# Seven block products in place of eight for the gate and up tiles of a float32 feed-forward on Trainium2

## Chip, cores and metric

The kernel runs on one core of one Trainium2 chip. The metric is device time in microseconds from start to end of one execution; the median of three runs is compared. Engines are called as in the profile: PE (TensorE matmuls), PEld (its weight loads), DVE (VectorE), ACT (ScalarE), POOL (GpSimd), SP (which issues the DMAs).

## What is computed

One block of an encoder: a feed-forward, token mixing (two attention branches, not touched here), a second feed-forward, a final norm. The part that matters:

```python
D_MODEL, SEQ, D_FF = 1024, 512, 2816      # all float32
def swiglu(h, w_in, w_down):
    g, u = jnp.split(h @ w_in, 2, axis=-1)
    return (jax.nn.silu(g) * u) @ w_down
...
h = modulate(rmsnorm(x, g_ffn2), sh3, sc3)
x = x + 0.5 * gt3[:, None, :] * swiglu(h, w_ffn2_in, w_ffn2_down)
return rmsnorm(x, g_final)
```

## The kernel before

Activations lie transposed, features on the 128 partitions, the 512 tokens along the free axis. `h` is eight K-tiles of 128 features (`KD` = 8). The 2816 inner features are 22 tiles (`NP_FF`), and each inner tile needs a gate tile and an up tile of 128 output features, a *pair*.

A float32 product runs as three matmuls (`mm3`): each operand is split into a high part, rounded by a cast on ACT (`wh_`, `f2h`, `hh`), and a low part, the rest, by a subtraction on DVE (`wl_`, `f2l`, `hl`); high*high, high*low and low*high add up in PSUM. So one output tile of `h @ w_in` over all 512 tokens (`proj`) is 8 K-tiles x 3 = 24 matmuls of 512 columns, and a pair is 48.

The second feed-forward (`swiglu(2, ...)`) goes like this. `first_group` makes the first `FIRST` = 3 pairs together, K-tile by K-tile, while `h` is still being formed, in halves of 256 tokens, into six PSUM banks. Then 19 pairs follow one by one: load 512 KB of gate weights (`ws_2g`) and 512 KB of up weights (`ws_2u`), split both, 48 matmuls, and `gated`: Silu on ACT, product on DVE, split into `hh` and `hl`. The inner tiles come in three groups (`THIRDS`: 8, 7 and 7). After each of the first two groups the eight output tiles (*down tiles*, weights `ws_2d`) are multiplied from the group's inner tiles and added to `x` by DVE. The last group's down tiles run in `residual`, the last four (`LAST`) in two halves of 256 tokens, followed by the sums of squares, the final norm and the output.

Nothing in the code is issued in the order in which it is written. `Plan` records all operations and a list scheduler orders them: an operation goes to its engine when its operands and a slot for its result are there, by its priority; `Plan.cost` estimates durations, `LAT` the delays between engines, `CAPS` how many buffers of a kind may live. Each engine then runs its list strictly in order, with semaphore waits. A bank serves one engine at a time. All operations are issued from one helper line, so rows are told apart by the names of tiles.

Of the kernel before, what the change touches and what calls it, by code (L numbers as in the profile page):

```python
# [30 lines left out]
THIRDS = ((0, 8), (8, 15), (15, 22))  # L31
# [15 lines left out]
# the work up to the end of the first projections, in the order of its urgency, and what engines wait for  # L47
# [18 lines left out]
WG_POOL = (1, 3)  # L66
RING = 2
# [3 lines left out]
CAPS = {"x": 4, "x2": 8, "sq": 4, "h": 16, "hid": 20, "sg": 1, "mt0": 2, "mt256": 2, "nrm": 6, "wst": 1, "whi": 7, "wlo": 7,  # L71
# [5 lines left out]
# the mixing: I index scores, A sparse queries, L latents, U latent values, R rotary queries, P query and key  # L77
# pairs, S and W scores and values of a latent head, T top-k, G gates, D and E scores and values of four sparse heads
# [5 lines left out]
# its operations in the order of their urgency, and what engines wait for  # L84
# [29 lines left out]
TINY = {"norm": 16, "top1": 2, "top2": 2, "top3": 2, "mla": 24, "dsa": 24}  # L114
# [14 lines left out]
def _mt(w):  # L129
    """(K, M) -> [M/128][128 partitions of K][K/128][128]"""  # L130
    k, m = w.shape
    return w.reshape(k // P, P, m // P, P).transpose(2, 1, 0, 3)


def _prep(inp):
# [9 lines left out]
    for n in (1, 2):  # L145
# [5 lines left out]
        for t, (lo, hi) in enumerate(THIRDS):  # L151
            a[f"w{n}d{t}"] = wd[:, :, lo:hi].reshape(KD, P, (hi - lo) * P)
# [28 lines left out]
    # rows that mask the first 64 queries of each block from its last 64 keys: queries, keys  # L181
# [20 lines left out]
class View:  # L202
# [31 lines left out]

    def bitcast(self, dt):
        return View(self.buf, self.chain + [("bitcast", dt)], self.p, self.off, self.dims, dt)
# [5 lines left out]
    def box(self):  # L242
        """partitions, columns, and the runs of columns where these have holes"""
# [11 lines left out]
    def real(self):  # L255
        ap = self.buf.base()
        for kind, *a in self.chain:
            if kind == "get":
                ap = ap[a[0]]
            elif kind == "bitcast":  # L260
                ap = ap.bitcast(a[0])
            else:
                ap = ap.rearrange(a[0], **a[1])
# [44 lines left out]
class Clock:  # L308
    """the tensor engine's clock: half as fast after a window in which it did little"""
# [21 lines left out]
# functions of ScalarE by the table that it loads for them  # L331
# [3 lines left out]
class Plan:  # L335
# [27 lines left out]
    def record(self, eng, nc_engine, fn, args, kw):  # L363
# [14 lines left out]
        if op.eng == "pe":  # L378
            # the share of the time in which rows of the array work
# [6 lines left out]
        op.step = self.step  # L386
        deps = {}
# [8 lines left out]
        for v in outs:  # L396
# [40 lines left out]
    def cost(eng, fn, outs, ins, kw, args):  # L437
        """an estimate, for the order alone"""
# [20 lines left out]
    # -- scheduling  # L459
    def order(self):  # L460
# [28 lines left out]
        while len(done) < len(self.ops):  # L489
            best = None  # L490
            for e, lst in ready.items():
# [4 lines left out]
                for op in lst:  # L496
# [4 lines left out]
                    for b in op.banks:  # L501
                        # a bank serves one engine at a time
# [9 lines left out]
                # an engine is not to begin something long just before urgent work  # L512
# [92 lines left out]
class Block:  # L605
# [8 lines left out]
    def small(self, kind, n=4):  # L614
        """per-partition scalars, from a ring of its own for each kind of use"""
# [11 lines left out]
    def later(self):  # L627
        """work that only fills what the rest leaves free"""
# [5 lines left out]
    def urgent(self, *engines):  # L634
        """work that all of the next work waits for"""
# [4 lines left out]
    def split(self, hi, lo, src, engine=None):  # L640
        """hi + lo == src: hi rounded to float32r by ScalarE, the rest by VectorE"""
# [12 lines left out]
    def mm3(self, ps, wh, wl, xh, xl, start, stop, hh=True):  # L654
        mm = self.nc.tensor.matmul
        if hh:
            mm(ps, wh, xh, start=start, stop=False)
        mm(ps, wh, xl, start=False, stop=False)
        mm(ps, wl, xh, start=False, stop=stop)

    def proj(self, w, x, nk, name, tag, cols=ALL):
        """one tile of 128 output features: sum over nk K-tiles"""
# [896 lines left out]
```

## Time and profile before

| | |
|---|---|
| median of three runs | 1181.84 us (1181.27 to 1186.75) |
| span of the profiled execution | 1182.4 us, 0.6 us above that median |
| PE busy, share of the span | 1137.4 us, 96% |
| PEld, DVE, ACT, POOL busy | 949.1, 744.1, 502.6, 123.3 us |
| HBM read / written | 148.11 / 13.63 MB |
| second feed-forward | from about 797 us to the end |

The busy share of PE is an average over stages, so the stretches have to be read by themselves. A matmul's printed duration reaches to its modelled end; back to back they overlap, and the distance from start to start is what counts. DVE and ACT instructions overlap a little in the same way.

### The profile page before, as it was taken

The page shows a single profiled execution, that of the slowest core. Times are in us where ns is not written, and L with a number is a line of the kernel's source. Part 1 is how long each engine was busy: PE and PEld are TensorE (multiplying, and loading weights), DVE is VectorE, ACT ScalarE, POOL GpSimd, SP SyncE. Part 2 cuts the span into 40 slices and gives each one's busy share as a digit, 9 for nine tenths or more (in the row PEclk, how much of TensorE's full clock was granted, in tenths as well). Part 3 has the DMA queues.
Part 4 walks back from the last instruction along what each step waited for, and adds up shares of the span by engine and source line. Part 5 has one row for each costly group of instructions (what it writes and reads, how often), then busy time and mean ns, then how long its engine had stood idle before and what let it go on. Part 6 is the DMA issues. An engine that isn't in the chain of part 4 may idle for free. (4 is left out here: it accounts for less than half of the span.)

```text
span 1182.4 us, 15861 instructions
## 1 busy us (share of the span) xinstructions
PE 1137.4 (96%) x5955; PEld 949.1 (80%) x5957; DVE 744.1 (63%) x1381; ACT 502.6 (43%) x896; POOL 123.3 (10%) x111
## 2 busy tenths in 40 slices
PE   5999999999999999988999999999999999999996
PEld 3878788887877899776888777889988888888886
DVE  8876665547664796899997786848433333333335
ACT  5562413423343256454768777524432222223220
POOL 5120000000000000021235352000000000000000
PEclk8899999999999999999999999999999999999998
DMA  8555566548545753221144256423322332333212
GB/s 292 188 182 180 171 225 194 175 166 271 182 152 184 264 172 121 72 81 65 55 127 123 95 190 209 157 68 112 107 97 99 92 105 78 100 107 100 83 32 71
DMA packets 64543, 163.88 MB, mean 139 GB/s; under 512 B 9762, under 2 KB 21538, under 8 KB 64467
## 3 DMA queue, kind: packets, MB, share of 16 engines
q1 hardware_dynamic: 64466, 162.88, 41.7%
q8 instruction: 46, 0.75, 0.3%
q14 instruction: 31, 0.25, 0.1%
HBM read 148.11 MB, written 13.63 MB: 137 GB/s over the span
## 5 line engine op out<-in xcount | busy, mean ns | idle before, releaser
L602 DVE CUSTOM_DVE_ANT_0 junk<-ada,sc,vecs 128x1024 bf16<-128x1024 f32 x66 | 84.5, 1281 | 28.6 <-DMA ada<-in_w_ada_dram 28.4
L602 PE MATMUL bank<-hmh,wh_ib 128*128 128x512 f32 x200 | 79.8, 400 | 1.7 <-ACT wh_ib L602 1.7
L602 PE MATMUL bank<-hmh,wl_ib 128*128 128x512 f32 x200 | 80.2, 404 | 0.3 <-POOL wl_ib L602 0.3
L602 PE MATMUL bank<-hml,wh_ib 128*128 128x512 f32 x200 | 79.5, 398 | 0.0
L602 DVE TENSOR_TENSOR wl_2d<-ws_2d,wh_2d 128x896 fp32r<-128x896 f32 (+1 forms) x24 | 27.3, 1137 | 75.2 <-ACT wh_2d L602 75.2
L602 PE MATMUL bank<-hl,wh_2d 128*128 128x512 f32 (+1 forms) x204 | 73.6, 361 | 0.0
L602 PE MATMUL bank<-hh,wh_2d 128*128 128x512 f32 (+1 forms) x204 | 73.5, 360 | 0.0
L602 PE MATMUL bank<-hh,wl_2d 128*128 128x512 f32 (+1 forms) x204 | 73.4, 360 | 0.0
L602 PE MATMUL bank<-hh,wh_1d 128*128 128x512 f32 (+1 forms) x197 | 72.6, 369 | 0.0
L602 PE MATMUL bank<-hl,wh_1d 128*128 128x512 f32 (+1 forms) x197 | 72.4, 367 | 0.0
L602 PE MATMUL bank<-hh,wl_1d 128*128 128x512 f32 (+1 forms) x197 | 72.2, 366 | 0.0
L602 DVE TENSOR_TENSOR wl_2g<-ws_2g,wh_2g 128x1024 fp32r<-128x1024 f32 x19 | 23.3, 1225 | 60.1 <-ACT wh_2g L602 60.1
L602 DVE SCALAR_TENSOR_TENSOR x<-bank,gt,x 128x512 f32<-128x512 f32 (+1 forms) x66 | 44.0, 666 | 25.5 <-PE bank L602 25.4
L602 PE MATMUL bank<-f1h,wh_1g 128*128 128x512 f32 x152 | 59.5, 391 | 0.0
L602 PE MATMUL bank<-f1l,wh_1g 128*128 128x512 f32 x152 | 59.2, 389 | 0.0
L602 PE MATMUL bank<-f1h,wl_1g 128*128 128x512 f32 x152 | 59.2, 389 | 0.0
L602 PE MATMUL bank<-f2h,wh_2g 128*128 128x512 f32 x152 | 59.1, 389 | 0.0
L602 PE MATMUL bank<-f2l,wh_2g 128*128 128x512 f32 x152 | 59.1, 389 | 0.0
L602 PE MATMUL bank<-f1h,wh_1u 128*128 128x512 f32 x152 | 59.1, 389 | 0.0
L602 PE MATMUL bank<-f1l,wh_1u 128*128 128x512 f32 x152 | 59.1, 389 | 0.0
L602 PE MATMUL bank<-f2h,wl_2g 128*128 128x512 f32 x152 | 59.1, 389 | 0.0
L602 PE MATMUL bank<-f2h,wh_2u 128*128 128x512 f32 x152 | 59.1, 389 | 0.0
(328 smaller groups left out, 3088.2 us busy)
## 6 DMA issues: line engine op xcount, KB each, us to landing
ada<-in_w_ada_dram SPq DMA_DIRECT2D x72, 512.0 KB, 4.5
ws_ib<-in_wib_dram SPq DMA_DIRECT2D x25, 512.0 KB, 3.4
ws_1g<-in_w1b_dram SPq DMA_DIRECT2D x19, 512.0 KB, 3.7
ws_1u<-in_w1b_dram SPq DMA_DIRECT2D x19, 512.0 KB, 3.5
ws_2g<-in_w2b_dram SPq DMA_DIRECT2D x19, 512.0 KB, 3.7
ws_2u<-in_w2b_dram SPq DMA_DIRECT2D x19, 512.0 KB, 3.4
ws_1d<-in_w1d_dram SPq DMA_DIRECT2D x16, 448.0 KB, 3.5
ws_2d<-in_w2d_dram SPq DMA_DIRECT2D x16, 448.0 KB, 3.2
```

What stands on the lines that cost most here:

```text
L602: op.fn(*[real(v) for v in op.args], **{k: real(v) for k, v in op.kw.items()})
```

## The change

Only the second feed-forward changes its arithmetic. A pair is seen as a 2x2 block product: rows gate and up, the sum over the first and the second four K-tiles (1 and 2 below), the tokens in two halves a and b. Winograd's form of Strassen's method makes its four results from seven block products, each 4 K-tiles x 3 = 12 matmuls of 256 columns, so 84 of them. It needs sums of the weight blocks (`wc_`: `s12`, `s34`, formed for each pair) and of the blocks of `h` (`f2t`, T0 to T3, formed once by `token_combinations`). Per pair four operands are split: the gate weights `a` (1024 columns), `t` = s34 (1024), `s` = s12 (1024) and `b` = the second up half (512). The products add up in two banks, A and C, with ACT copying intermediate sums of A to SBUF (`v`, `v2`) between products, and DVE adding or subtracting to get `g` and `u`.

Further: the K-tiles of the first group go 0, 4, 1, 5, ..., without the six opening matmuls over all 512 columns; pair loads wait for a matmul of the third K-tile (`fast_from`); five groups of inner tiles (4, 4, 4, 5, 5); a group's eight down tiles are recorded between the pairs of the next group. In the planner, the cost of an unnamed float32r matmul becomes 13.4 ns + columns / 2.4, which can also shift the order in the first feed-forward.

```diff
-THIRDS = ((0, 8), (8, 15), (15, 22))
+GROUPS = {1: ((0, 8), (8, 15), (15, 22)), 2: ((0, 4), (4, 8), (8, 12), (12, 17), (17, 22))}
...
+FAST_FROM = 2
...
+        if eng == "pe" and op.step is None and mv.dt == F32R:
+            op.cost = 13.4 + mv.n / 2.4
...
+        ks = [k // 2 + KD // 2 * (k % 2) for k in range(KD)] if fast is not None else list(range(KD))
...
+                    behind = halves[i][-2] if fast is not None else None
...
+                        if fast is not None:
+                            self.mm3(first[m][:w, cols], wh[:, c], wl[:, c], xh, xl, start, k == ks[-1] and cols.stop == S,
+                                     skip_group_check=True)
+                            continue
...
+            if fast is not None and k == ks[FAST_FROM]:
+                self.fast_from = nc.last_pe
+        if fast is not None:
+            for k in range(KD // 2):
+                fast.append(self.token_combinations(f"{name}t{k}", site, k, kept[k], kept[k + KD // 2]))
...
+        V.tensor_tensor(t13[:, 0], m0[:, a], m0[:, b], op=ALU.subtract)
+        V.scalar_tensor_tensor(t13[:, 1], m0[:, b], d, m1[:, b], op0=ALU.subtract, op1=ALU.subtract)
+        V.scalar_tensor_tensor(t24[:, 0], t13[:, 1], sh0, m0[:, a], op0=ALU.subtract, op1=ALU.subtract)
+        V.scalar_tensor_tensor(t24[:, 1], m1[:, a], sh1, t24[:, 0], op0=ALU.add, op1=ALU.add)
+        out = []
+        for i, t in enumerate((t13, t24)):
+            hi, lo = (self.g(f"{name}{c}{i}", F32R, shape=(P, 2, S // 2), tag="th") for c in "hl")
+            self.split(hi, lo, t)
+            out += [(hi[:, e], lo[:, e]) for e in range(2)]
...
+        with nc.after(self.fast_from):
+            nc.sync.dma_start(w0, src0)
+            nc.sync.dma_start(w21, src1[:, lo_])
+            nc.sync.dma_start(w22, src1[:, hi_])
...
+        p0 = parts("a", w0, "w")
+        V.tensor_tensor(s34[:, lo_], w0[:, lo_], w21, op=ALU.add)
+        V.tensor_tensor(s12[:, hi_], w21, w22, op=ALU.add)
+        V.tensor_tensor(s12[:, lo_], s12[:, hi_], w0[:, lo_], op=ALU.add)
+        V.tensor_tensor(s34[:, hi_], w0[:, hi_], s12[:, lo_], op=ALU.add)
+        p34 = parts("t", s34, "w")
+        p12 = parts("s", s12, "w")
+        p22 = parts("b", w22, "v")
+        A, C = (self.bank(f"{n}_{name}", "mm") for n in "ac")
...
+            for k in range(K4):
+                self.mm3(ps, *w[k], *x[k], start and k == 0, k == K4 - 1, skip_group_check=True)
...
+        product(A[:, a], cols(p0, 0), quarter(0, 0), True)
+        nc.scalar.copy(v[:, 0], A[:, a])
+        product(C[:, a], cols(p34, 0), T[1], True)
+        product(A[:, a], cols(p12, 0), T[2])
+        nc.scalar.copy(v[:, 1], A[:, a])
+        product(C[:, b], cols(p0, S), quarter(K4, 0))
+        product(A[:, a], cols(p12, S), T[0])
+        nc.scalar.copy(v2[:, 0], A[:, a])
+        V.tensor_tensor(g[:, 0], v[:, 0], C[:, b], op=ALU.add)
+        V.tensor_tensor(u[:, 1], v2[:, 0], C[:, a], op=ALU.subtract)
+        product(A[:, a], cols(p34, S), quarter(K4, 1))
+        product(C[:, a], cols(p22, 0), T[3])
+        V.tensor_tensor(u[:, 0], v[:, 1], C[:, a], op=ALU.subtract)
+        return g, u, A[:, a]
...
+        def gated_fast(i):
+            src = A[f"w{n}b"][i - FIRST]
+            g, u, c12 = self.fast_pair(f"f{i}", src[0], src[1], h, combos)
+            nc.scalar.activation(g[:, 0], g[:, 0], AF.Silu)
+            nc.scalar.activation(g[:, 1], c12, AF.Silu)
+            nc.vector.scalar_tensor_tensor(g, u, -1.0, g, op0=ALU.mult, op1=ALU.mult)
+            hi, lo = self.g(f"hh{n}_{i}", F32R, tag="hid"), self.g(f"hl{n}_{i}", F32R, tag="hid")
+            e = lambda t: t.rearrange("p (e t) -> p e t", e=2)
+            nc.scalar.copy(e(hi), g)
+            nc.vector.tensor_tensor(e(lo), g, e(hi).bitcast(F32), op=ALU.subtract)
+            hid[i] = (hi, lo)
...
+            for j, i in enumerate(new):
+                hidden(i)
+                while before and len(before) > KD - KD * (j + 1) // len(new):
+                    before.pop(0)()
...
+                before = [lambda d=d, tile=tile, weights=weights: tile(d, weights(d)) for d in range(KD)]
```

Three places show what the planner makes of it. Rows are in the order in which an engine runs them; the wait of an instruction stands behind it.

First, PE where one output ends and the next begins. Before, the up tile of pair 4 ends in one bank and the gate tile of pair 5 starts in another:

```order
L602 MATMUL bank0_179<-f2h7_7911,wh_2u4_7977 128x512
L602 MATMUL bank0_179<-f2l7_7931,wh_2u4_7977 128x512
L602 MATMUL bank0_179<-f2h7_7911,wl_2u4_7989 128x512
L602 MATMUL bank7_186<-f2h0_6715,wh_2g5_8010 128x512 [waits Activation_49]
L602 MATMUL bank7_186<-f2l0_7661,wh_2g5_8010 128x512
L602 MATMUL bank7_186<-f2h0_6715,wl_2g5_8024 128x512
```

Now, in pair 8, the fifth product (`f8s`) ends in bank 188, three matmuls of a down tile follow in bank 183, and the sixth product (`f8t`) goes on in bank 188:

```order
L612 MATMUL bank5_188<-f2t3h0_8072,wh_f8s_8892 128x256
L612 MATMUL bank5_188<-f2t3l0_8089,wh_f8s_8892 128x256
L612 MATMUL bank5_188<-f2t3h0_8072,wl_f8s_8911 128x256
L612 MATMUL bank0_183<-hh2_4_8470,wh_2d1_0_8928 128x512
L612 MATMUL bank0_183<-hl2_4_8481,wh_2d1_0_8928 128x512
L612 MATMUL bank0_183<-hh2_4_8470,wl_2d1_0_8936 128x512 [waits DVE_49]
L612 MATMUL bank5_188<-f2h4_7669,wh_f8t_8829 128x256 [waits Activation_49]
L612 MATMUL bank5_188<-f2l4_7681,wh_f8t_8829 128x256
```

The sixth product waits for ACT, which first has to copy the fifth sum out of the same bank; the three down matmuls stand between.

Second, DVE while the first group runs, just before the first pair. Before, it makes the low parts of `h` and of the weights of pairs 3 to 5:

```order
L602 SCALAR_TENSOR_TENSOR f2l7_7931<-mf2h7_0_7902,mod_73,f2h7_7911 128x256 [waits Activation_49]
L602 SCALAR_TENSOR_TENSOR f2l7_7931<-mf2h7_256_7908,mod_73,f2h7_7911 128x256 [waits Activation_49]
L602 TENSOR_TENSOR wl_2u3_7943<-ws_2u3_7868,wh_2u3_7924 128x1024 [waits DMAHW1_49,PE_49,Activation_49]
L602 TENSOR_TENSOR wl_2g4_7962<-ws_2g4_7898,wh_2g4_7950 128x1024 [waits DMAHW2_49,PE_49,Activation_49]
L602 TENSOR_TENSOR wl_2u4_7989<-ws_2u4_7934,wh_2u4_7977 128x1024 [waits DMAHW3_49,PE_49,Activation_49]
L602 TENSOR_TENSOR wl_2g5_8024<-ws_2g5_7972,wh_2g5_8010 128x1024 [waits DMAHW4_49,DVE_49,Activation_49]
```

Now it is at the last block sums of `h` (`f2t3`) and the weight sums of pair 3 (`wc_f30` is s12, `wc_f31` is s34), and the product `sg2_0` of the first group's first pair stands ahead of `wl_f3t`, which the second product of pair 3 needs:

```order
L612 TENSOR_TENSOR wc_f31_8101<-ws_f30_7914,ws_f31_7924 128x512 [waits DMAHW2_49,PE_49]
L612 TENSOR_TENSOR wc_f30_8110<-ws_f31_7924,ws_f32_7932 128x512 [waits DMAHW3_49,PE_49]
L612 TENSOR_TENSOR f2t3l1_8118<-f2t32_8083,f2t3h1_8104 128x512 [waits Activation_49]
L612 TENSOR_TENSOR wc_f30_8110<-wc_f30_8110,ws_f30_7914 128x512 [waits DVE_49]
L612 TENSOR_TENSOR wl_f3b_8132<-ws_f32_7932,wh_f3b_8003 128x512
L612 TENSOR_TENSOR wc_f31_8101<-ws_f30_7914,wc_f30_8110 128x512 [waits DVE_49]
L612 TENSOR_TENSOR sg2_0_8137<-sg2_0_8137,bank6_189 128x512 [waits PE_49,Activation_49]
L612 TENSOR_TENSOR wc_f41_8157<-ws_f40_7939,ws_f41_7950 128x512 [waits DMAHW5_49,DMAHW4_49]
L612 TENSOR_TENSOR wl_f3t_8170<-wc_f31_8101,wh_f3t_8150 128x1024 [waits Activation_49]
```

Twenty-eight operations on 256 columns and further ones, counted in the prediction, stand between the first multiplication of `x` by the second half's norm and this last row.

Third, DVE in a later pair, where before it had four operations a pair. Now, while pair 7 is multiplied:

```order
L612 TENSOR_TENSOR g_f7_8895<-v_f7_8850,bank2_185 128x256 [waits PE_49,Activation_49]
L612 TENSOR_TENSOR wl_f8s_8911<-wc_f80_8784,wh_f8s_8892 128x1024 [waits PE_49,Activation_49]
L612 TENSOR_TENSOR u_f7_8924<-v2_f7_8913,bank2_185 128x256 [waits Activation_49]
L612 TENSOR_TENSOR wl_2d1_0_8936<-ws_2d1_0_8897,wh_2d1_0_8928 128x512 [waits DMAHW7_49,PE_49,Activation_49]
L612 TENSOR_TENSOR wc_f90_8951<-ws_f91_8614,ws_f92_8622 128x512 [waits DMAHW1_49,DVE_49]
L612 TENSOR_TENSOR wl_f9b_8960<-ws_f92_8622,wh_f9b_8944 128x512 [waits Activation_49]
L612 TENSOR_TENSOR u_f7_8924<-v_f7_8850,bank2_185 128x256 [waits PE_49]
L612 TENSOR_TENSOR wc_f90_8951<-wc_f90_8951,ws_f90_8748 128x512 [waits DVE_49]
L612 SCALAR_TENSOR_TENSOR g_f7_8895<-u_f7_8924,g_f7_8895 128x512 [waits DVE_49]
L612 TENSOR_TENSOR wc_f91_8875<-ws_f90_8748,wc_f90_8951 128x512 [waits DVE_49]
L612 SCALAR_TENSOR_TENSOR x2_6_6927<-bank1_184,gt_75,x2_6_6927 128x512 [waits PE_49]
L612 TENSOR_TENSOR hl2_7_8988<-g_f7_8895,hh2_7_8980 128x512 [waits Activation_49]
```

The parts of pair 8 and the sums of pair 9 are made in between, one pair or two ahead of PE.

## Rows read from the trace of the kernel before

**Rows 1.** Cores: span and mean granted clock.
```profile
core 0: 1182.4 us, clock 0.988
```

**Rows 2.** Stretches: length; PE, PEld, DVE, ACT, POOL busy (instructions); clock; DMA; GB/s.
```profile
790.00:841.10 51.10, 51.10 (x412) 50.35 (x411) 34.39 (x80) 21.39 (x34) 0.00 (x0) 1.00 0.34 104
841.10:1160.00 318.90, 318.90 (x1454) 266.10 (x1453) 113.93 (x130) 86.38 (x107) 0.00 (x0) 1.00 0.27 88
...
1160.00:1170.20 10.20, 10.20 (x86) 10.07 (x84) 7.93 (x27) 1.25 (x3) 0.00 (x0) 1.00 0.15 51
1170.20:1182.40 12.20, 1.96 (x8) 1.02 (x6) 5.78 (x21) 0.42 (x1) 0.00 (x0) 0.63 0.38 129
```

**Rows 3.** Waits from 800 to 1160: us in total, times, longest us.
```profile
DVE wl_2d L602 <- ACT wh_2d L602: 75.2, 24, 4.5
...
ACT wh_2g L602 <- DMA ws_2g<-in_w2b_dram: 57.0, 19, 4.5
```

**Rows 4.** Timeline of PE, 822 to 841: start us, us, what.
```profile
821.79 0.28 PE L602 MATMUL bank<-f2l,wh_f 128*128 128x256 f32 x1
...
840.99 0.28 PE L602 MATMUL bank<-f2h,wl_f 128*128 128x256 f32 x1
841.11 0.40 PE L602 MATMUL bank<-f2h,wh_2g 128*128 128x512 f32 x1
```

**Rows 5.** Timeline of PE, 910 to 955.
```profile
909.82 0.39 PE L602 MATMUL bank<-hh,wh_2d 128*128 128x512 f32 x1
...
954.25 0.39 PE L602 MATMUL bank<-f2l,wh_2g 128*128 128x512 f32 x1
```

**Rows 6.** Groups by shape, PE from 841 to 1171: busy us, mean ns.
```profile
L602 PE MATMUL bank<-f2h,wh_2g 128*128 128x512 f32 x152 | 59.1, 389 | 0.0
...
L602 PE MATMUL bank<-hh,wh_2d 128*128 128x512 f32 x148 | 57.6, 389 | 0.0
```

**Rows 7.** Groups by shape, DVE from 795 on: busy us, mean ns, idle before.
```profile
L602 DVE TENSOR_TENSOR wl_2g<-ws_2g,wh_2g 128x1024 fp32r<-128x1024 f32 x19 | 23.3, 1225 | 60.1 <-ACT wh_2g L602 60.1
...
L602 DVE TENSOR_TENSOR hl<-sg,hh 128x512 fp32r<-128x512 f32 x22 | 15.2, 692 | 13.7 <-ACT hh L602 13.7
...
L602 DVE SCALAR_TENSOR_TENSOR x<-bank,gt,x 128x512 f32<-128x512 f32 x20 | 14.9, 746 | 9.0 <-PE bank L602 9.0
...
L602 DVE TENSOR_TENSOR acc_n<-acc_n,sq_n 128x256 f32<-128x256 f32 x12 | 5.1, 423 | 2.4 <-ACT sq_n L602 2.3
```

**Rows 8.** Timeline of DVE, 792 to 850 and at the end.
```profile
814.21 0.87 DVE L602 SCALAR_TENSOR_TENSOR mf2h<-x,a,bank 128x256 f32<-128x256 f32 x2 [0.59 <-PE bank L602]
...
816.07 1.26 DVE L602 SCALAR_TENSOR_TENSOR mf2h<-x,a,bank 128x256 f32<-128x256 f32 x3
...
1175.74 3.22 DVE L602 SCALAR_TENSOR_TENSOR o<-x,vecs,bank 128x256 f32<-128x256 f32 x8 [1.31 <-PE bank L602]
```

**Rows 9.** Groups by shape, ACT: busy us, mean ns, idle before.
```profile
L602 ACT CAST wh_2g<-ws_2g 128x1024 fp32r<-128x1024 f32 x19 | 19.9, 1050 | 57.0 <-DMA ws_2g<-in_w2b_dram 57.0
...
L602 ACT CAST pBh<-bank 128x256 fp32r<-128x256 f32 x8 | 3.0, 374 | 6.3 <-PE bank L602 5.2 <-DVE tiny_dsa L602 1.0
```

**Rows 10.** Timelines, hand-offs: PE to ACT, then ACT to PE.
```profile
857.23 0.39 PE L602 MATMUL bank<-f2h,wl_2g 128*128 128x512 f32 x1
...
857.66 0.60 ACT L602 ACTIVATE sg<-bank 128x512 f32<-128x512 f32 x1 [1.07 <-PE bank L602]
...
530.94 1.04 ACT L602 CAST wh_ib<-ws_ib 128x1024 fp32r<-128x1024 f32 x1
...
532.03 0.50 PE L602 MATMUL bank<-hmh,wh_ib 128*128 128x512 f32 x1 [1.67 <-ACT wh_ib L602]
532.37 0.39 PE L602 MATMUL bank<-hml,wh_ib 128*128 128x512 f32 x1
```

**Rows 11.** Timeline of ACT, 836 to 845.
```profile
839.51 0.60 ACT L602 ACTIVATE sg<-bank 128x512 f32<-128x512 f32 x1 [1.10 <-PE bank L602]
```

**Rows 12.** DMA issues after 700: count, KB each, median us to landing.
```profile
ws_2g<-in_w2b_dram SPq DMA_DIRECT2D x19, 512.0 KB, 3.7
```

More of the change, by code (lines that the diff above doesn't have):

```diff
@@ L764, in residual, with modulated, first_group @@
         return r
-    def modulated(self, h, x, r, a, sh, cols):
+    def modulated(self, h, x, r, a, sh, cols, kept=None, behind=None):
         nc = self.nc
-        hi, lo = (t[:, cols] for t in h)
-        t = self.g(f"m{h[0].name}_{cols.start}", shape=(P, cols.stop - cols.start), tag=f"mt{cols.start}")
-        nc.vector.scalar_tensor_tensor(t, x[:, cols], a, r[:, cols], op0=ALU.mult, op1=ALU.mult)
+        hi, lo = h
+        t = kept[:, cols] if kept is not None else self.g(f"m{h[0].buf.name}_{cols.start}", shape=(P, cols.stop - cols.start), tag=f"mt{cols.start}")
+        with nc.after(behind, True):
+            nc.vector.scalar_tensor_tensor(t, x[:, cols], a, r[:, cols], op0=ALU.mult, op1=ALU.mult)
         nc.scalar.activation(hi, t, AF.Identity, bias=sh)
-        nc.vector.scalar_tensor_tensor(lo, t, sh, hi.bitcast(F32), op0=ALU.add, op1=ALU.subtract)
-    def first_group(self, name, site, r, src, n, widths, before=None, w0=None):
+        return nc.vector.scalar_tensor_tensor(lo, t, sh, hi.bitcast(F32), op0=ALU.add, op1=ALU.subtract)
+    def first_group(self, name, site, r, src, n, widths, before=None, w0=None, fast=None):
         nc = self.nc
         first = [self.bank(f"{name}_{m}", "mm") for m in range(len(widths))]
-        h = []
+        h = [None] * KD
         at = lambda what: nc.at(("", "h", "g")[site] + what)
-        for k in range(KD):
+        ks = [k // 2 + KD // 2 * (k % 2) for k in range(KD)] if fast is not None else list(range(KD))
+        kept, halves = {}, [[None, None], [None, None]]
+        for j, k in enumerate(ks):
             with at(f"w{k}"):
                 wh, wl = w0 if w0 and not k else self.weights(
-                    src[k], f"{name}{k}", n, engine=nc.gpsimd if not site and k in W0_POOL else None)
+                    src[k], f"{name}{k}", n,
+                    engine=nc.gpsimd if not site and k in W0_POOL else None)
             if before:
@@ L800, in first_group @@
                         start = k == 0 and cols.start == 0
+                        if fast is not None:
+                            self.mm3(first[m][:w, cols], wh[:, c], wl[:, c], xh, xl, start, k == ks[-1] and cols.stop == S,
+                                     skip_group_check=True)
+                            continue
                         if start:
[L802 to L803 removed]
+                            nc.tensor.matmul(first[m][:w], wh[:, c], h[0][0][2], start=True, stop=False)
@@ L804, in first_group @@
+                        self.mm3(first[m][:w, cols], wh[:, c], wl[:, c], xh, xl,
                                  False, k == KD - 1 and cols.stop == S, not start)
-        return first, h
+            if fast is not None and k == ks[FAST_FROM]:
+                self.fast_from = nc.last_pe
+        if fast is not None:
+            for k in range(KD // 2):
+                fast.append(self.token_combinations(f"{name}t{k}", site, k, kept[k], kept[k + KD // 2]))
+            return first, h
+        return first, [tuple(part[2] for part in hk) for hk in h]
@@ new lines, in fast_pair, with parts, product @@
+    def fast_pair(self, name, src0, src1, h, t):
+        nc = self.nc
+        V = nc.vector
+        a, b = HALVES
+        half = S // 2
+        K4 = KD // 2
+        lo_, hi_ = slice(0, S), slice(S, D)
+        w0 = self.g(f"ws_{name}0", shape=(P, D), tag="fst")
+        w21, w22 = (self.g(f"ws_{name}{i}", shape=(P, S), tag="vst") for i in (1, 2))
+        with nc.after(self.fast_from):
+            nc.sync.dma_start(w0, src0)
+            nc.sync.dma_start(w21, src1[:, lo_])
+            nc.sync.dma_start(w22, src1[:, hi_])
+        s12, s34 = (self.g(f"wc_{name}{i}", shape=(P, D), tag="wct") for i in range(2))
+        def parts(n, t, tag):
+            hi, lo = (self.g(f"w{c}_{name}{n}", F32R, shape=t.shape, tag=tag + ("hi" if c == "h" else "lo")) for c in "hl")
+            self.split(hi, lo, t)
+            return hi, lo
+        p0 = parts("a", w0, "w")
[7 more added lines that the diff above has]
+        A, C = (self.bank(f"{n}_{name}", "mm") for n in "ac")
+        cols = lambda hs, at: [(hs[0][:, at + k * P:at + k * P + P], hs[1][:, at + k * P:at + k * P + P]) for k in range(K4)]
+        def product(ps, w, x, start=False):
+            for k in range(K4):
+                self.mm3(ps, *w[k], *x[k], start and k == 0, k == K4 - 1, skip_group_check=True)
+        quarter = lambda k0, e: [(h[k0 + k][0][e], h[k0 + k][1][e]) for k in range(K4)]
+        T = [[t[k][i] for k in range(K4)] for i in range(4)]
+        g, u, v, v2 = (self.g(f"{n}_{name}", shape=(P, 2, half), tag=t) for n, t in (("g", "g4"), ("u", "g4"), ("v", "sv"), ("v2", "sv")))
+        product(A[:, a], cols(p0, 0), quarter(0, 0), True)
[12 more added lines that the diff above has]
+        return g, u, A[:, a]
@@ L949, in tile @@
                     fill()
-            if t < 2:
-                for d in range(KD):
-                    tile(d, weights(d))
+            return tile, weights
+        groups = GROUPS[n]
+        before = []
+        for t, (i0, i1) in enumerate(groups):
+            new = range(max(i0, FIRST), i1)
+            for j, i in enumerate(new):
+                hidden(i)
+                while before and len(before) > KD - KD * (j + 1) // len(new):
+                    before.pop(0)()
+            tile, weights = down(t, i0, i1)
+            if t < len(groups) - 1:
+                before = [lambda d=d, tile=tile, weights=weights: tile(d, weights(d)) for d in range(KD)]
+                if n == 1:
+                    for step in before:
+                        step()
+                    before = []
         return self.residual(f"n{n + n // 2}", tile, weights, LAST if n == 2 else SPLIT)
```

75 lines of the change are left out of this document (50 added, 25 removed).

## Prediction

> **What bounds the kernel now.** I read the cores first: one core, mean granted clock 0.988 [rows 1], so the clock has little to give. Then the stretches [rows 2], because the page's busy share is an average over stages. From 790 to 1160 us PE is busy for the whole of each stretch at clock 1.00. DVE is busy 113.93 and ACT 86.38 of 318.9 us in the pairs' stretch. Only the last 12.2 us are not PE's. The list of waits [rows 3] asks the opposite question, who stands idle: DVE waits 75.2 us for casts and ACT 57.0 us for loads, and PE is in no row of it. So the second feed-forward is PE's from 790 to 1170 us, its length is the number of matmuls times their pitch, and DMA, DVE and ACT are covered. The change takes matmul columns away and spends DVE and ACT time, so I need PE's pitch at the two widths and the price of the new dependences.
>
> The pitch comes from starts, since printed durations overlap. At 256 columns, in the first group: (841.11 - 821.79) / 161 = 0.1200 us [rows 4]. At 512 columns: (954.25 - 909.82) / 196 = 0.2267 us, over pairs and down tiles [rows 5]. The groups print 389 ns for both kinds of 512-column matmul [rows 6], so they are one price. Both pitches lie 13.4 ns above columns / 2.4 GHz: a matmul has a fixed cost, and the new form issues more matmuls.
>
> **The change, part by part.**
>
> *Pairs.* Before, 48 x 0.2267 = 10.88 us. Now 84 x 0.1200 = 10.08 us. Seven eighths of 10.88 would be 9.52; but 84 matmuls are 42 more than seven eighths of 48, and their fixed costs, 42 x 13.4 ns = 0.56, leave 0.80 of the 1.36 us. 19 pairs: **-15.2**.
>
> Here the Trainium skill would count otherwise. The rows say that a matmul costs 13.4 ns beyond its columns [rows 4, 5]. "TensorE: Matmul & The Clock Gate", section "Wait — 56ns, not 53.3ns?", puts the distance of matmuls at full clock at N / 2.4 GHz plus about 2.5 ns. An estimate by that page is 48 x 215.8 - 84 x 109.2 = 1.19 us a pair, 22.5 us in all. The trace disagrees at both widths, and I go by it.
>
> A 256-column matmul leaves little room for its weights: in the first group's stretch PEld is busy 50.35 of 51.10 us [rows 2]. Yet the pitch there is the 0.1200 that I use, with weights changing from matmul to matmul just as in the seven products. So a weight load adds nothing beyond it.
>
> *First group.* Six opening matmuls of 512 columns become 256 columns wide: 6 x (0.2267 - 0.1200) = **-0.6**. The order of its K-tiles costs PE nothing: same matmuls.
>
> *Groups of inner tiles.* The down tiles keep their 22 x 8 x 3 = 528 matmuls of 512 columns, but the last four tiles of the last group run in halves. With 7 inner tiles that is 168 x 0.1200 + 444 x 0.2267 = 120.8 us for all of them, with 5 it is 120 x 0.1200 + 468 x 0.2267 = 120.5: **-0.3**.
>
> The ideal sum is -16.1. Now what is spent.
>
> *DVE and ACT load.* DVE per pair before: two low parts of 1024 columns at 1.225, a product of 512 (about a low part, 0.69) and `hl` 0.692 [rows 7], 3.83 us. Now three low parts of 1024 (3.68), one of 512 and four weight sums of 512 (five at 0.692, 3.46), three additions from PSUM of 256 (1.27 at 0.423), product and `hl` (1.38): 9.8 us. The 40 down tiles take a low part and an addition to `x` each, 0.692 + 0.746 = 1.44. Together 19 x 9.8 + 40 x 1.45 = 244 us of some 312, 78%. In a cycle of one pair and two down tiles PE has 10.08 + 24 x 0.2267 = 15.5 us and DVE 9.8 + 2.9 = 12.7. ACT has per pair three casts at 1.050 [rows 9], one of half that width, three copies of 256 (0.374 each, the nearest row, also out of PSUM), two Silu and one cast for `hh`: about 6.3 us. Both fit, and the order shows parts made about a pair ahead of PE. Loads: 512 KB lands in 3.7 us [rows 12] and the bytes of a pair are unchanged. I price the load at 0, covered by PE's stream; without that cover see the second rival.
>
> *The new waits between products.* Bank A holds three intermediate sums that ACT has to copy before PE writes there again. The distance is one end of PE's pitch to ACT's start, 0.20 us (last matmul starts 857.23, its pitch ends 857.46, ACT starts 857.66), the copy 0.374, and 0.05 from ACT's end to PE's start (531.98 to 532.03) [rows 9, 10]: 0.63 us. If PE does arrive early, its first matmul after the wait takes 0.34 instead of 0.23 [rows 10], 0.11 more. For the first two copies a product of 12 x 0.1200 = 1.44 us on bank C lies between: slack 0.8. For the third, `v2`, the sixth product follows in the same bank, and the planner puts three 512-column down matmuls between, 0.68 us. That is 0.05 of slack, so each pair pays between 0 and 0.11: 0 to 2.1 us for 19. I take the middle, **+1.0**. Behind such a wait on PE's queue stand the sixth product and everything after it, so it goes to the end in full. The same copy waits if ACT is inside a cast of 1.05 us when the sum is ready; that is the first rival.
>
> *Startup of the pairs.* The first pair now needs the sums of `h` and of weights, when DVE is also forming the second half of `h`. From 814.21 us, where the second half begins [rows 8], it has 28 operations of three inputs on 256 columns at 0.40 (1.26 for three from 816.07, 3.22 for eight at 1175.74 [rows 8]), 4 x 0.423 of two inputs, `sg2_0` of 512 columns and 15 more of them at 0.692, and 2 of 1024 at 1.225 [rows 7]: 11.2 + 1.7 + 11.1 + 2.5 = 26.5, so 840.7 if none overlaps, and a little earlier since neighbours do. But the cast before `wl_f3t` lies on ACT behind the first Silu of the first group, which ran at 839.51 for 0.60 [rows 11]: 840.1 + 1.05 + 1.14 gives about 842.3 for `wl_f3t`. PE ends the first group near 841.1 - 0.6 = 840.5 and has one product, 1.44, and a third of the next matmul group before it needs this tile: about 842.2. Even, then. The third product's parts follow on DVE behind that, one more low part and a sum later, at 842.3 + 1.2 + 0.7 = 844.2; PE needs them after two products and the three leading matmuls of a third, 844.0 to 844.2. Pairs 3 and 4 come equally tight, so between 0 and 4; nearest to the even case: **+1.0**. Loads of pair 3 wait for the first group's third K-tile, some 149 matmuls before its end (822.6), and land by 826.3, before they are split.
>
> *Tail.* Second half shorter and three more `o` operations behind it (0.40 each): 0 to 1.2 on the 12.2 us of [rows 2]. I take **+0.3**.
>
> Sum: -16.1 + 1.0 + 1.0 + 0.3 = -13.8. The profiled span of 1182.4 becomes 1168.6; it is 0.6 above the median, and I give the median scale as 1168.5, as profiles vary by more than that rest.
>
> **Rivals.**
>
> *ACT copies late (first rival).* The 57 copies sit in one strict queue with casts of 1.05 us. If each arrives on average 0.29 us past its cover, that is 57 x 0.29 = 16.5 us, the whole gain; half as much gives 1176. For it: slack of 0.05 at `v2`. Against: two of three have 0.8 us, and ACT is busy about half of the time. 1172 to 1183; chance 0.17, half of it still faster by 0.5%.
>
> *DVE becomes the pace (other side).* Each low part stands behind a cast of its own high part. If DVE, whose list is strict, stood idle for each of four casts (3 x 1.05 + 0.62 = 3.77) and for PE's results, a cycle would be 12.7 + 3.8 + 0.6 = 17.1 against PE's 15.5: 19 x 1.6 = 30 us more, 1196. It decides where DVE's idle time exceeds 2.8 us per pair with its down tiles. For it: DVE already waits 75.2 us for 24 down casts [rows 3], 3.1 each. Against: there it waits because it has nothing else, and the order now puts other sums between cast and low part. Chance 0.07.
>
> *The change does not do what it says.* The planner's new cost of a matmul reaches the first feed-forward and may reorder it; the rows moved there are few. 3 us either way on top of the sum, 1165 to 1172 or worse by one late stage: chance 0.08.
>
> *The fixed cost is 2.5 ns, not 13.4.* Products at 109 ns would give about 1160. The rows deny it: chance 0.02.
>
> **How the numbers follow.** The forecast with its own bounds (0 to 2.1, 0 to 4, 0 to 1.2 against 2.3 taken) has 0.66 and gives 1166.3 to 1173.6. This kernel's runs tell about 0.5%, 5.9 us, from no change, so faster means under 1175.9. Faster: 0.66, half of the late copies, 0.085, nearly all of the reordering, 0.08, and 0.02, together 0.85. Slower: the DVE case, 0.07. Same: 0.08, the other half of the late copies. For 8 in 10 the range leaves out the DVE case, the end of the late copies and the lowest part: 1164.5 to 1177.
>
> **What would show it.** Right: starts of `f`-products 0.120 us apart; PE's waits in the second feed-forward under 4 us in all, the largest at `f*t` behind ACT and at pair 3; PE's end near 1157; a tail of 12 to 13 us; DVE busy near 80% of the pairs' stretch without a PE wait for it. Wrong: PE waiting for `wl_f..` of DVE in every pair (the DVE case), ACT copies starting 0.5 us or more after their product (the first rival), or a pitch above 0.125 where weights change every matmul beside a busy DVE and ACT.

## Result and the profile after

The changed kernel takes 1172.32 us in the median of six runs (1171.02 to 1178.48), against 1181.92 for the kernel before on the same chip: ratio 0.992, 95% interval 0.9898 to 0.9941. In a second comparison on another occasion it is 1172.17 against 1184.90, 0.9903 (0.9884 to 0.9921). It is faster by 0.8 to 1.0%, inside the stated range and 3.8 us above the forecast of 1168.5.

The windows of the changed kernel: length; PE, PEld, DVE, ACT, POOL busy (instructions); clock; DMA share; GB/s.

```profile
790.00:841.70 51.70, 51.70 (x417) 51.00 (x417) 42.59 (x105) 22.85 (x41) 0.00 (x0) 1.00 0.30 103
841.70:1150.00 308.30, 308.15 (x2141) 287.07 (x2140) 227.69 (x333) 140.48 (x239) 0.00 (x0) 1.00 0.30 91
1150.00:1156.50 6.50, 6.50 (x55) 6.42 (x53) 5.30 (x20) 1.25 (x3) 0.00 (x0) 1.00 0.01 3
1156.50:1170.30 13.80, 2.47 (x12) 1.54 (x10) 8.11 (x27) 0.42 (x1) 0.00 (x0) 0.62 0.44 153
```

As in [rows 2], PE is busy for all of the first three, but for 0.15 us. DVE has twice the work, 227.69 of 308.30 us or 74%, and PE does not wait for it. The list of PE's waits from 780 us on is short; its first two rows belong to the tail:

```profile
PE bank L612 <- DVE o L612: 3.7, 1, 3.7
PE bank L612 <- ACT sq_n L612: 0.6, 1, 0.6
PE bank L612 <- ACT v_f L612: 0.2, 1, 0.2
```

From PE's timeline (start, duration, what), the borders of the stages: the last matmul of the mixing's output, the first of pair 3, and the last of a down tile.

```profile
805.49 0.28 PE L612 MATMUL bank<-yh,wl_out 128*128 128x256 f32 x1
...
841.72 0.28 PE L612 MATMUL bank<-f2h,wh_f3a 128*128 128x256 f32 x1
...
1156.40 0.28 PE L612 MATMUL bank<-hh,wl_2d 128*128 128x256 f32 x1
```

In the timeline of before, these matmuls start at 804.22, 841.11 [rows 4] and 1170.05 us. The differences of such starts, in us:

| stage | before | changed | forecast | measured |
|---|---|---|---|---|
| all ahead of the second feed-forward | 804.22 | 805.49 | 0 | +1.3 |
| first group | 36.89 | 36.23 | -0.6 | -0.7 |
| pairs and down tiles | 328.94 | 314.69 | -15.2 - 0.3 + 1.0 + 1.0 = -13.5 | -14.3 |
| tail, to the end of the span | 12.32 | 13.88 | +0.3 | +1.6 |
| span | 1182.4 | 1170.3 | -13.8 | -12.1 |

The stage of pairs came out slightly better than forecast. The loss lies at its two ends: 1.3 us ahead of it and 1.3 us more in the tail. The tail repeats (13.88 and 13.89 us in two profiles of the changed kernel). The first row does not: in the fourteen profiles of this case that stretch takes 799.55 to 810.27 us, so 1.3 us between two profiles show no cause by themselves. The experiments ask for the causes.

### The profile page after: what moved, and what is told of

Its sections match the earlier page's. It is cut to its first block, busy times and chain, and to the rows that moved or that the text cites. A ratio compares the mean times of both kernels' runs of the same rounds, so it can differ in the third digit from the quotient of the medians.

```text
span 1170.3 us, 17656 instructions
## 1 busy us (share of the span) xinstructions
PE 1123.1 (96%) x6617; PEld 966.1 (83%) x6617; DVE 865.5 (74%) x1612; ACT 557.7 (48%) x1034; POOL 124.0 (11%) x110
## 5 line engine op out<-in xcount | busy, mean ns | idle before, releaser
L612 DVE SCALAR_TENSOR_TENSOR x<-bank,gt,x 128x512 f32<-128x512 f32 (+1 forms) x82 | 56.0, 683 | 28.8 <-PE bank L612 28.7
L612 PE MATMUL bank<-f1h,wl_1u 128*128 128x512 f32 x152 | 59.1, 389 | 0.0
L612 DVE TENSOR_TENSOR wl_1d<-ws_1d,wh_1d 128x896 fp32r<-128x896 f32 (+1 forms) x24 | 27.3, 1136 | 36.1 <-ACT wh_1d L612 20.8
L612 ACT CAST wh_1d<-ws_1d 128x896 fp32r<-128x896 f32 (+1 forms) x24 | 23.5, 978 | 62.4 <-DMA ws_1d<-in_w1d_dram 54.9
L612 POOL TENSOR_TENSOR wl_ib<-ws_ib,wh_ib 128x1024 fp32r<-128x1024 f32 x16 | 38.9, 2434 | 131.6 <-ACT wh_ib L612 96.8
L612 ACT CAST wh_2d<-ws_2d 128x512 fp32r<-128x512 f32 (+1 forms) x40 | 26.5, 663 | 43.2 <-DMA ws_2d<-in_w2d_dram 24.7
L612 ACT ACTIVATE sq_n<-x 128x256 f32<-128x256 f32 (+1 forms) x35 | 17.5, 508 | 59.4 <-DVE x L612 56.8
```

The lines of the kernel that those rows point to most:

```text
L612: op.fn(*[real(v) for v in op.args], **{k: real(v) for k, v in op.kw.items()})
```

## Experiments

Ratios are to the kernel before, run on the same chip.

### What a matmul of 256 columns costs

```diff
-pg = self.proj(wg, h, KD, ...)
+pg = self.proj_halves(wg, h, KD, ...)    # second feed-forward: each matmul as two of 256 columns; pu too
...    # proj_halves itself is left out here
```

> The kernel before with each pair's 48 matmuls of 512 columns issued as 96 of 256 columns, all else kept: eight block products instead of seven, without sums. By the pitches of the rows (0.1200 and 0.2267) a pair takes 96 x 0.1200 - 48 x 0.2267 = 0.64 us more, 19 pairs 12.1, median about 1194.5. Rival (fixed cost 2.5 ns): 0.13 us a pair, 2.4 in all, median about 1185.

1196.89 us, ratio 1.011 (1.0083 to 1.0138). From the first pair to the last down matmul 341.14 us, 12.2 more than before. In PE's timeline of this run:

```profile
850.11 0.28 PE L602 MATMUL bank<-f2h,wl_2u 128*128 128x256 f32 x1
...
889.95 0.28 PE L602 MATMUL bank<-f2l,wh_2g 128*128 128x256 f32 x1
```

332 intervals in 39.84 us: 0.1200 us, as in the first group [rows 4]. Halving the width without saving a product costs 12.2 us, 12.1 expected, so the fixed 13.4 ns are real. By the Trainium skill's page "TensorE: Matmul & The Clock Gate", section "Wait — 56ns, not 53.3ns?", an estimate would be 48 x 2.5 ns x 19 = 2.3 us; no run here agrees with that, and the measurement decides.

### The planner's cost line and the order in the first feed-forward

The change also alters the estimate of a matmul's cost everywhere. One kernel is before with this line alone, the other is the changed kernel with the line valid only in the second feed-forward.

```diff
 # before, one line added
+if eng == "pe" and op.step is None and mv.dt == F32R: op.cost = 13.4 + mv.n / 2.4
 # changed kernel
-if eng == "pe" and op.step is None and mv.dt == F32R:
+if self.fine and eng == "pe" and op.step is None and mv.dt == F32R:    # fine: set when swiglu(2) begins
```

> The kernel before with the planner's new cost of a matmul and nothing else; the second feed-forward keeps its eight products. On DVE's list the load-bound product of ada then stands ahead of wl_1d in the first feed-forward, as in the changed kernel. Theory (order): PE waits about 2.0 us for t5m near 280 us, as in the changed kernel's trace, and the median is 1 to 2.5 us above before. Rival (chance of one execution): the load was late by itself; no wait above 0.5 us at that place and the median within 0.5 us of before.

> The changed kernel with the new matmul cost valid only from the second feed-forward on, so that the first feed-forward and the mixing are issued in the order of before (plus four tiny_shift operations). Theory (order): the wait of 2.0 us for t5m goes, the second feed-forward starts 1 to 2 us earlier, median 1170.3 to 1171.3, against 1172.3 for the change. Rival: median within 0.5 us of the change.

The line alone: 1184.45 us, ratio 1.0006 (0.999 to 1.0022), too wide to tell theory from rival. The change without it in the first feed-forward: 1169.63 us, 0.9892 (0.9876 to 0.9907), 0.7 us below the expected range. Its profile has no wait of PE between 270 and 290 us. PE near 280 us in the changed kernel; the bracket holds the idle time before and what ended it:

```profile
276.15 2.37 PE L612 MATMUL bank<-t5m,t5w 128*32 128x384 bf16 x48
280.57 0.37 PE L612 MATMUL bank<-t5m,t5w 128*32 128x448 bf16 x2 [2.04 <-DVE t5m L612]
280.87 0.50 PE L612 MATMUL bank<-hh,wh_1d 128*128 128x512 f32 x1
```

And PE in the kernel with the old order there:

```profile
278.24 0.50 PE L613 MATMUL bank<-hh,wh_1d 128*128 128x512 f32 x1
...
330.14 0.96 PE L613 MATMUL bank<-t5m,t5w 128*32 128x448 bf16 x13
```

Two matmuls of `t5m` have moved ahead by 50 us: in the old order they stand with eleven others at 330.14, in the new order at 280.57, ahead of down matmuls and before DVE has made their `t5m`. PE's list is strict, so it waits. On DVE's list a row has moved too, as the expectation of the line alone says: the product `junk<-ada`, which waits for a load, now stands ahead of `wl_1d`. That is not what PE waits for. In the kernel with the line alone, where PE's wait is 1.6 us, DVE has caught up and itself waits for a cast just ahead of `t5m`:

```profile
278.55 1.09 DVE L604 TENSOR_TENSOR wl_1d<-ws_1d,wh_1d 128x896 fp32r<-128x896 f32 x1 [0.18 <-ACT wh_1d L604]
279.56 1.60 DVE L604 TENSOR_SCALAR t5m<-posf,thr 128x448 bf16<-128x448 f32 x4
```

The order as a whole was taken back by experiment and the wait went; that it is these two rows is read from the traces. From the first gate matmul of the first feed-forward to its last up matmul it takes 298.67 us in all six profiles with the old order (before, the split pairs, the five groups alone, this kernel, the two with both repairs) and 300.39 to 302.49 in all eight with the new one. So the order costs 1.7 us or more at this place, whichever arithmetic follows.

How much of it reaches the end no single comparison tells: the interval of the line alone holds zero, and in its profile the second feed-forward begins as early as before (804.22 us in both). The medians of all kernels together tell more. The second feed-forward repeats within 0.4 us between two profiles of one kernel, so its change can be taken from the profiles and subtracted from the change of the median; the rest is an estimate of what is lost ahead of it. With the new order that is 0.3 to 3.7 us in eight comparisons, 2.4 in the mean, with the old order -0.8 to 0.7 in five, 0.1 in the mean. About 2 us reach the end, then, though the two ranges overlap.

### The tail: one bank for two halves

```diff
 r = self.bank(f"r_{name}", "rn")
+rs = [r, self.bank(f"r2_{name}", "t5") if name == "n3" else r]
...
-self.rms(norm, r, cols)
+self.rms(norm, rs[i], cols)    # and the o operations read r[i]; the returns are left out here
```

> The changed kernel with one edit: the second half of the final norm has a PSUM bank of its own, so that PE's last two dg_n matmuls need not wait until DVE has read the first half's norm for all eight o operations. Theory (shared bank): the wait of 3.7 us on DVE's o at the end falls to about 2.5, the tail from 13.4 to about 12.2 us, median 1.0 to 1.4 us below the change. Rival: DVE's three o operations still stand in its list ahead of what is needed (the second half's o follow them), so the time stays within 0.4 us.

1171.73 us, 0.9915 (0.9896 to 0.9935): 0.6 us below the change, which was measured on another occasion, and too little for these intervals. The traces are clear. The changed kernel, DVE and PE in order of time:

```profile
1160.69 1.26 DVE L612 SCALAR_TENSOR_TENSOR o<-x,vecs,bank 128x256 f32<-128x256 f32 x3
...
1162.01 1.22 PE L612 MATMUL bank<-dg_n,ones 128*128 128x256 f32 x2 [3.69 <-DVE o L612]
```

With a bank for each half, PE's same matmuls:

```profile
1161.72 1.22 PE L612 MATMUL bank<-dg_n,ones 128*128 128x256 f32 x2 [2.51 <-DVE dg_n L612]
```

The releaser changes from `o` to `dg_n` and the wait is 1.18 us shorter. The tail falls from 13.88 to 12.69 us. The first half's `o` operations read the bank that PE is about to write, and the last three of them stood between. That is 1.19 of the 1.56 us that the tail has grown by.

Whether the seven products or the five groups bring this about is told by the groups alone:

```diff
-THIRDS = ((0, 8), (8, 15), (15, 22))
+GROUPS = {1: ((0, 8), (8, 15), (15, 22)), 2: ((0, 4), (4, 8), (8, 12), (12, 17), (17, 22))}
```

> The kernel before, eight products kept, with the five groups of inner tiles (4, 4, 4, 5, 5) alone. PE from the first pair to the last down tile: 329.2 us less 0.3 by the columns. Theory (shared bank): the last halves last 12 matmuls of 256 less per tile, DVE's eight o operations of the first half are no longer done when PE wants the bank, and the tail grows from 12.1 to 13.0 to 13.5 us; span and median 0.5 to 1.2 us above before. Rival (the tail of the changed kernel comes from its seven products): tail within 0.3 us of 12.1.

1185.52 us, 1.0011 (0.9993 to 1.003), not to be told from before. Its tail is 13.50 us, 1.18 more than before, and PE's wait is the same:

```profile
PE bank L602 <- DVE o L602: 3.7, 1, 3.7
```

So the smaller last group does it: less PE work in the second half covers fewer `o` operations. The other 0.4 us of the changed kernel's tail lie behind the last `o`: 3.8 us to the end of the span there and with the bank of its own, 3.4 before and in the groups alone; their cause was not followed. The stage of pairs gained more than forecast, 328.18 against 328.94 us, -0.8 instead of -0.3. The rest is the border of the stage: four norm matmuls of two columns (`ones,acc_n`, 0.5 us), which before stand ahead of the last down matmul, now stand behind it.

### The cover of the third copy

```diff
-nc.scalar.copy(v2[:, 0], A[:, a])
+quick = nc.scalar.copy(v2[:, 0], A[:, a])
+quick.quick, quick.cost = 1.0, 10.0    # for the planner alone: 10 ns, and at PE at once
...    # the planner's lines that read `quick` are left out here
```

> The changed kernel, where the planner is told that the third copy out of bank A (v2) takes 10 ns and reaches PE at once. In nine of the 19 pairs the sixth product then stands one 512-column matmul behind the fifth, in the others three or more. By the rows a copy needs 0.20 + 0.37 + 0.05 = 0.62 us and that cover is 0.23, so each of the nine waits 0.40 and pays up to 0.11 at its first matmul: 3.5 to 4.6 us above the change, in PE's waits on ACT v_f. Rival (the hand-off is hidden elsewhere): within 1 us of the change.

1181.01 us, 0.9975 (0.9961 to 0.999). First the change at pair 9, PE and ACT in order of time:

```profile
936.82 0.28 PE L612 MATMUL bank<-f2t3h,wl_f9s 128*128 128x256 f32 x1
...
937.14 0.37 ACT L612 COPY v_f<-bank 128x256 f32<-128x256 f32 x1 [0.20 <-PE bank L612]
...
937.64 0.31 PE L612 MATMUL bank<-f2h,wh_f9t 128*128 128x256 f32 x1
```

The fifth product's pitch ends at 936.94; the copy ends at 937.51, and the sixth product starts at 937.64, after three down matmuls. 0.13 us passes between copy and PE, where 0.05 is needed: a slack of 0.08, where the forecast had 0.05. With one down matmul between, in the kernel of this experiment:

```profile
944.72 0.28 PE L612 MATMUL bank<-f2t3h,wl_f9s 128*128 128x256 f32 x1
944.84 0.39 PE L612 MATMUL bank<-hh,wh_2d 128*128 128x512 f32 x1
945.46 0.38 PE L612 MATMUL bank<-f2h,wh_f9t 128*128 128x256 f32 x1 [0.23 <-ACT v_f L612]
945.68 0.28 PE L612 MATMUL bank<-f2l,wh_f9t 128*128 128x256 f32 x1
```

0.62 us from the fifth product's end to the sixth, 0.39 more than the pitch of the down matmul, and 0.10 more at the first matmul after it (0.22 instead of 0.12): close to the terms of the prediction. The total is larger than expected, 322.38 us against 314.69 from the first pair on, +7.7 instead of 3.5 to 4.6, because all 19 pairs pay and not nine. In the other ten ACT is inside another instruction when the product ends and starts the copy 0.41 to 1.03 us after it, and PE always starts 0.05 us behind the copy. The first rival's mechanism, ACT late with a copy, therefore exists: against products that never wait, the ten pairs cost about 4.0 us and the nine about 4.5.

In the changed kernel the third copy is late as well in six of the 19 pairs (0.61 to 1.03 us after its product), but there the planner put five to seven down matmuls between. The one wait on `v_f` in the changed kernel's list is not behind a third copy. It is behind the first copy of pair 13, which ACT starts late, at the end of a cast of 1.05 us:

```profile
992.54 0.38 PE L612 MATMUL bank<-f2t0h,wh_f13s 128*128 128x256 f32 x1 [0.15 <-ACT v_f L612]
```

### Does DVE become the pace?

```diff
+for _ in range(5):    # 9 in the second kernel; in the third 5 from pair 6 on, else 1
     V.tensor_tensor(s34[:, lo_], w0[:, lo_], w21, op=ALU.add)
```

> The changed kernel with one weight sum of 512 columns computed five times instead of once per pair, which adds 4 x 0.69 = 2.8 us of DVE time a pair, 52 in all, and changes no result. DVE's busy time in the pairs' stretch goes from 74% to about 91%. Theory (PE keeps the pace as long as DVE's work fits): 0 to 4 us above the change, PE waits under 4 us in that stretch. Rival (DVE's idle time behind casts is needed, so the pace is DVE's as soon as it has under 2.8 us idle per pair): 10 us or more above.

> The same with nine copies of the sum: 5.5 us of DVE time a pair, 105 in all. With 227 us busy now in 308, DVE would need about 330: it is the pace by either theory. Theory: the stretch is 20 to 35 us longer, DVE near 98% busy, PE waits for wl_f or wc_f of DVE. Rival (idle time behind casts adds to it): 45 us or more.

Five copies: 1180.30 us, 0.9969 (0.9956 to 0.9981), 322.37 us from the first pair to the last down matmul, 7.7 more. Nine: 1202.55 us, 1.0151 (1.0121 to 1.0181), 345.07 us, 30.4 more. For five copies that is neither the theory's 0 to 4 us nor the rival's 10 or more. The windows of that run show where it comes from (columns as above):

```profile
842.00:846.00 4.00, 1.91 (x16) 1.71 (x15) 3.31 (x6) 2.21 (x6) 0.00 (x0) 1.00 0.61 183
846.00:850.00 4.00, 2.02 (x7) 1.73 (x8) 4.00 (x6) 4.00 (x6) 0.00 (x0) 0.66 0.04 16
850.00:855.00 5.00, 5.00 (x28) 5.00 (x28) 5.00 (x8) 0.73 (x2) 0.00 (x0) 0.59 0.00 0
855.00:1120.00 265.00, 264.50 (x1857) 247.35 (x1857) 239.50 (x365) 123.85 (x210) 0.00 (x0) 1.00 0.31 96
```

From 855 us on DVE is busy 90% and PE misses 0.5 us, that too in pair 3. All of the loss lies at this pair: PE waits, and then works for some 7 us at the lower clock level of 1.2 GHz (granted clock 0.66 and 0.59 in those two windows). Its list of waits in the pairs' stretch:

```profile
PE bank L612 <- ACT wh_f3t L612: 3.6, 1, 3.6
PE bank L612 <- ACT v_f L612: 0.5, 1, 0.5
PE bank L612 <- DVE wl_f3t L612: 0.5, 1, 0.5
```

Why `wh_f3t` is late shows in DVE's timeline of that run:

```profile
838.61 0.69 DVE L612 TENSOR_TENSOR wc_f<-ws_f,ws_f 128x512 f32<-128x512 f32 x1
842.69 0.69 DVE L612 TENSOR_TENSOR sg<-sg,bank 128x512 f32<-128x512 f32 x1 [3.39 <-ACT sg L612]
843.29 0.69 DVE L612 TENSOR_TENSOR wc_f<-ws_f,ws_f 128x512 f32<-128x512 f32 x1
```

The last sums of pair 3 now stand behind `sg2_0`, which waits 3.39 us for a Silu. The Silu is late because ACT's table load of 1.28 us, which the changed kernel has at 835.80 in idle time, here stands behind the wait for the bank, at 840.76. So it was the order of the lists again, with DVE idle just ahead of PE's wait, and the last run moves the added load past the start:

> The changed kernel with the same four more sums of 512 columns as in the run with five copies, but only from the fourth pair (pair 6) on: 16 x 2.8 = 44 us more of DVE time, which changes no result. There, all 7.7 us of the loss lay at pair 3 (waits of 3.6 and 0.5 us, then PE at half clock for 6.83 us). Theory (only the start is tight, the later pairs have DVE time to spare): from the first pair to the last down tile 314.5 to 315.5 us as in the change, no wait at wh_f3t, DVE about 88% busy. Rival (DVE's load itself costs): 318 us or more with waits for wl_f or wc_f in later pairs.

1172.88 us, 0.991 (0.9886 to 0.9933), and 314.51 us from the first pair to the last down matmul, 314.69 without the added work. DVE is busy 88% of 855 to 1120 us and PE misses nothing:

```profile
855.00:1120.00 265.00, 264.99 (x1861) 247.83 (x1860) 234.09 (x355) 123.18 (x211) 0.00 (x0) 1.00 0.30 96
```

The rival falls as it was put: its limit of 2.8 us idle time per pair does not exist, since 88% busy leaves about 1.9 us per pair and PE loses nothing. That sums of the next pair fill the time behind casts is read from the order.

Of the 30.4 us that nine copies lose, 13.5 lie at pair 3 again (a wait of 10.2 us, then the lower clock). The other 16.9 lie behind it, where DVE is busy 98%:

```profile
862.00:1120.00 258.00, 249.94 (x1714) 231.94 (x1713) 254.13 (x396) 111.81 (x192) 0.00 (x0) 0.98 0.29 92
```

The total is inside the theory's 20 to 35 us. PE's waits are not for DVE's `wl_f` or `wc_f`, as expected, but for ACT: its casts (`wh_f..`), which in turn wait for DVE's sums, and its copies (`v_f`, 3.7 us).

### Both repairs together

The matmul cost from the second feed-forward on, and the bank of its own.

> Both edits of the two runs before this one in one kernel. If both terms are real and independent: 2.2 to 3.2 us below the change, 1169.1 to 1170.1 median, span about 1167.6. If the order in the first feed-forward is worth nothing, 1171; if the bank is worth nothing, 1170.8.

> The changed kernel again, on the chip of the run after this one, so that the two are compared directly. The second feed-forward from its first pair to the last down tile 314.9 to 315.1 us, tail 13.3 to 13.6; ratio to before 0.990 to 0.993.

> The kernel with both edits again (matmul cost only from the second feed-forward, a bank of its own for the second half of the final norm). If the two terms are 2.2 and 1.2 us and nothing else differs: 3 to 4 us below the run ahead of this one, ratio to before 0.987 to 0.989. Rival (the first run of it was lucky in the mixing stage and the order is absorbed there): within 2 us of the run ahead.

First 1167.22 us, 0.9864 (0.9848 to 0.9881), better than expected; then 1170.52 us, 0.9885 (0.9867 to 0.9902), beside 1172.17 for the change, so that the second time the rival's words (within 2 us) hold. The change's own tail was 13.89 us, not 13.3 to 13.6. With both repairs it is 12.42 and 12.48 us in the two profiles, so 1.4 us are gained there. The 2.2 us of the first feed-forward are there in both (298.67 us), but in the second profile they are given back behind it. The windows from 410 to 420 us of the first profile, then of the second:

```profile
410.00:416.00 6.00, 5.79 (x49) 5.59 (x48) 5.53 (x21) 2.35 (x5) 0.00 (x0) 1.00 0.17 62
416.00:420.00 4.00, 4.00 (x32) 3.81 (x32) 3.74 (x9) 1.32 (x4) 0.00 (x0) 1.00 0.47 163
```

```profile
410.00:416.00 6.00, 3.98 (x33) 3.77 (x32) 5.97 (x15) 2.09 (x5) 1.00 (x2) 1.00 0.36 124
416.00:420.00 4.00, 4.00 (x23) 4.00 (x22) 2.41 (x12) 0.69 (x2) 0.00 (x0) 0.57 0.20 70
```

In the second, PE waits 2.0 us for the norm's `acc_n` and then has a granted clock of 0.57. The same kernel does either. The first profile is of the fastest of its four executions (1164.62 us), the second of the slowest of its six (1172.97). The wait is not the old order's alone: 1.4 us or more stand there in five of the fourteen profiles, two of them with the new order. What decides was not tested and stays open. That the version with both repairs beats the change by more than the 1.4 us of the tail is suggested by the first comparison and by the medians together, and not shown by the second comparison.

## Why the prediction was right, and where it was not

*Pitch.* -15.2 for the pairs rests on 0.1200 and 0.2267. Right: in the changed kernel 69 intervals from 841.72 to 850.00 us are 0.1200 each, and the split kernel confirms the price from the other side. The rival with a fixed cost of 2.5 ns is refuted.

*First group and groups of inner tiles.* -0.7 for -0.6, and -0.8 for -0.3 (groups alone), 0.5 of it by the border of the stage.

*Hand-off of `v2`.* The parts (0.20, 0.37, 0.05, and 0.10 at the next matmul) were right. Its size, +1.0, was a guess between 0 and 2.1. The third copy makes no wait that the list shows, but the first matmul behind it takes 0.149 to 0.222 us instead of 0.12 in 14 of the 19 pairs, 0.6 us in all. Another 0.5 us are paid behind first copies, in pairs 13 and 16, where the forecast had 0.8 us of slack and priced nothing. That the two come near +1.0 is luck in part. With the startup term the stage paid 15.2 + 0.8 - 14.3 = 1.7 of the 2.0 taken; the rest is spread over hundreds of starts in parts of a few ns.

*Startup of the pairs.* Called even, and it is: `wl_f3t` runs from 841.95 to 843.17 us on DVE, and PE's first matmul with it starts at 843.39. It cost nothing visible, where +1.0 was taken; with four more sums it cost 7.7. This was the tightest place of the change. In that run the wait came with DVE idle for 3.39 us just ahead, so from the order of the lists and not from the amount of DVE's work alone.

*Tail.* The step "0 to 1.2 ... I take +0.3" failed in its size: +1.6. I had counted the three `o` operations as work of DVE, but they hold the bank, so all of their 1.2 us stood between the last scaling and PE. The sign "a tail of 12 to 13 us" did not come. The stages' errors offset each other: 0.8 us better in the pairs and 0.1 in the first group, 1.3 worse in the tail, so -13.4 us from the first group to the end where -13.8 was forecast; that this is so close is luck.

*Ahead of the second feed-forward.* The step that the planner's cost would move "few" rows and nothing in the likeliest case failed: two rows moved ahead on PE's list made a wait of 2.0 us. It had been carried as a rival of 3 us with chance 0.08.

*Scale.* The step "it is 0.6 above the median, and I give the median scale as 1168.5" set a span beside a time. The time of the changed kernel's profiled execution, 1172.1 us, is 1.8 above its span of 1170.3. By that the profiled execution of before took about 1184.2 us (an estimate) and was itself slower than its median by some 2 us. The forecast hardly moved by it: the median 1181.9 less 13.8 is 1168.1. But it hides a loss in the table of stages. The medians fell by 9.6 us, and 13.4 were gained from the first group to the end, so nearly all of the 3.8 us by which the forecast was low lies ahead of the second feed-forward. In the second comparison the medians fell by 12.7 us, and 0.3 lies there.

*DVE as the pace.* Right to give it 0.07, for a reason that the runs now show: DVE at 88 to 90% costs PE nothing in the later pairs.

*Signs.* One sign of being wrong came and was too loose: ACT copies 0.5 us or more after their product, in six pairs. PE is covered there. Of the waits that were to be the largest, at `f*t` and at pair 3, none came.

## What to carry to other kernels

Count matmuls as well as columns: one eighth fewer columns promised 1.36 us a pair here, and the smaller matmuls left 0.80. An edit of a scheduler's cost reaches stages that the change doesn't touch, so compare the order of every engine's list there, and look for a row that has moved ahead of others while its operand still comes late. When the work between two users of a bank shrinks, ask which reads of the bank are still to come.

## What the runs showed of the hardware

A wait cost more than its length where the clock fell behind it: in the run with five copies the waits for pair 3 (3.6 and 0.5 us) came with granted clocks of 0.66 and 0.59 over 9 us, and the stage lost 7.7 us. The return from ACT to PE was 0.05 us in each of the 19 pairs with a short cover, whatever stood ahead of the copy. A 256-column matmul keeps its 0.1200 us with DVE 90% busy beside it.
